# Middle block's sample as half of a sixth pair, path A's low halves split on chip, W_B's sums in pieces, and last gates whose sums are not kept

## The chip, the cores and the metric

The kernel runs on one core of a Trainium2 chip. The metric is the device time of one execution in microseconds (us). Times of the kernel before are from three runs and from one profiled execution.

## What is computed

One layer over 2048 prompt tokens and 64 sample tokens with a state of their own, all in fp32: two paths from one input projection, merged by gates, then an output projection and a gate of 256 extra features.

```python
vA, bA, cA, zA, q, f, iv, zB, gA, gB = split_cols(rms_norm(x, g_pre) @ w_in)
u = cA * vA                                    # path A: a convolution of width 3
yA = (silu(zA) * bA * causal_conv3(u_ext, conv_w)) @ w_a_out
fg = lb + (1.0 - lb) * sigmoid(f)              # path B: 8 heads of 128 x 128
S_new, o = hgrn2_scan(S0, silu(q) * QK_SCALE, 1.0 - fg, iv, log(fg))
yB = (rms(o) * g_onorm * silu(zB)) @ w_b_out
merged = sigmoid(gA) * yA + sigmoid(gB) * yB
x = x + rms_norm(merged @ w_o, g_post)
gate = sigmoid(rms_norm(x, g_ple) @ w_ple_gate)
x = x + (p @ w_ple_proj) * gate
```

The scan goes in chunks of 64 tokens: within a chunk an attention with a causal mask, between chunks a state of 128 x 128 that decays by a factor for each key channel. The outputs are x, the convolution's tails and the states, for prompt and sample apart.

## The kernel before

**Blocks.** The 2112 tokens (prompt 0 to 1407, the 64 sample tokens, then the rest of the prompt) are worked off in three blocks of 768, 704 and 640 tokens. Features stand on the partitions. The middle block holds ten chunks of prompt and, as its eleventh and last, the sample.

**Matrix multiplications.** An fp32 factor is split into a high part (a cast to fp32r) and a low part (the rest), and a product is three multiplications: hi by xhi, hi by xlo, lo by xhi (lines 442, 443, 444 in `sgroup`). `sgroup` makes two columns of weights by two halves of a block with seven products instead of eight. It needs seven weight blocks of 128 x 512: A11, A12 and A22, which are parts of the weights, and four sums S1 to S4. A product is 12 multiplications. Behind each product `hook()` runs one piece of other work, taken from a list of slots.

**Weights.** In the first block `combined` loads the parts, forms the four sums on VectorE (DVE, line 352), makes the casts on ScalarE (ACT) and the low halves on DVE (line 226), and `keep_sum` and `split_w` store the sums (S) and the low halves (low) to HBM. Later blocks read them back: `kept_w` loads a block (raw) and `split_w` makes the cast on ACT and loads the low half, both in the queue of SyncE (SP). `used_later` lists which low halves are stored. `prepare_sums` does the same for weights of later stages, by DMAs of POOL (GpSimd): it loads four blocks, forms S1, S3, S2, S4 and stores each with its low half. For W_B, the weights of path B's output, this runs beside path A of the middle block, one pair of columns in each of the steps j = 3 to 7 (`side`).

**Stages of a block.** Path B (8 heads), then the gates, path A (8 steps j, each with the groups VA/CA and ZA/BA), the two output projections with the merge, W_O and the last gate. The gates' group GB + 6 is the last of the list `fills`; in the middle block it comes first of all, in block 2 behind the preparation of head 5 (`late_gates`).

**A head.** `head_prep` makes two `sgroup`s: forget gate and values (FF, IV), then z and queries (ZB, QQ), with the scan of the logarithms and the keys `ka` and `kb` between. v, the keys `kb` and the output `on` are turned to tokens on partitions: a transposition of 32 x 32 blocks on DVE (line 1054), a write to DRAM by POOL (tv, tk, to; line 1056), a read in another order (line 1061), and for tk a copy on POOL (line 1066). `head_attn` then makes, in slots between the products of the next group: the scores p_a (lines 1111 and 1112), the mask (1120), the update p_u = kt v (1126), the states one after another (1143), the output p_o (1166 and 1168) and its norm. Two chunks of 64 make a pair, and four pairs share a PSUM bank. In the blocks after the first, slots 2 and 3 hold p_a of the two parts, 6 p_u, 8 p_o. The middle block's lone sample chunk goes by itself, in slots 4, 5, 7 and 10, through tiles `lone` and by transpositions on TensorE: of keys and values (1098), and of the output (1193).

**Order.** Instructions of an engine run in the order in which they are recorded; each DMA queue takes its transfers in order as well. The names in the rows below are tiles with a running number: pg is a gemm's PSUM bank, pa one of the attention, r and hf tiles of a whole and a half block, raw, hi, lo and s weight blocks.

Of the kernel before, what the change touches and what calls it, by code (L numbers as in the profile page):

```python
# [18 lines left out]
P = 128  # L19
# [28 lines left out]
def plan():  # L48
# [3 lines left out]
    for size in SIZES:  # L52
# [8 lines left out]
        assert all(g["len"] == 2 * CH for g in groups[:npair])  # L61
        parts = [groups[i : min(i + 4, npair)] for i in range(0, npair, 4)] + [[g] for g in groups[npair:]]
        halves = [dict(t0=t0 + o, off=o, n=size // 2) for o in (0, size // 2)]
        out.append(dict(t0=t0, n=size, runs=runs, npair=npair, parts=parts, groups=groups, segs=halves, last=t0 + size == TOK))
# [29 lines left out]
def hybrid_step(  # L94
# [102 lines left out]
    lone = [const.tile([P, 1, P], F32, tag=f"lone{i}", name=f"lone{i}") for i in range(3)]  # L197

    def constants():
# [9 lines left out]
        for t in atts + lone:  # L209
            V.memset(t, 0.0)  # L210
# [474 lines left out]
    def rstd_of(ms_ap, out_ap, scale, start=0):  # L685
# [3 lines left out]
        powers[:] = [G.tensor_tensor(out_ap, out_ap, mhalf[start : start + shape[0], :].to_broadcast(shape), ALU.pow).ins]  # L689
# [246 lines left out]
    def head_prep(bl, hc, hd, first, hs, before):  # L936
        n, npair = bl["n"], bl["npair"]
        nch, np1 = n // CH, npair * P
        sf, vt = rt(), rt()

        def sink_f(c, h, x, y):
# [9 lines left out]
            into(half(vt, h)[:, n1:], x[:, n1:], None if y is None else y[:, n1:])  # L951
# [5 lines left out]
        lg, b, eq, qx = rt(), rt(), rt(), rt()  # L957
        wrote = [turned("tv", vt, qx, npair)]
# [8 lines left out]
        ka, kb, qe, z = hf(npair * CH), rt(), rt(), rt()  # L967

        def scaled(after):
# [17 lines left out]
            more = npair - 2 * SWAP  # L987
            for lo, hi, to in (
                (0, SWAP, ka3[:, more + 1 :: 2, :]),
                (SWAP, 2 * SWAP, ka3[:, more : npair - 1 : 2, :]),  # L990
                (2 * SWAP, npair, ka3[:, :more, :]),
            ):
                own = slice(2 * lo, 2 * hi, 2)
                V.tensor_tensor(to, chunks(sf)[:, own, :], chunks(lg)[:, own, :], ALU.mult)
                scale = f2[:, lo:hi].unsqueeze(2).to_broadcast([P, hi - lo, CH])
                place = slice(2 * lo + (hi <= SWAP), 2 * hi, 2)
                V.tensor_tensor(chunks(kb)[:, place, :], to, scale, ALU.mult)
# [36 lines left out]
        with behind_all([*wrote, *powers]):  # L1034
            by_token = [in_rows("tv", npair)]
            if before is not None and not first:
                before["ot"] = in_rows("to", npair, before["on"])
            if not first:
                by_token.insert(0, in_rows("tk", npair))
        return dict(  # L1040
            eq=eq, f=f, ka=ka, kb=kb, qe=qe, qx=qx, vt=vt, z=z, by_token=by_token, on=None,
            npair=npair, more=npair - 2 * SWAP, first=first, last=bl["last"], carry=None,
# [26 lines left out]
    def head_attn(ip, gs, d, hd):  # L1069
# [3 lines left out]
        nt, ln = len(gs), gs[0]["len"]  # L1073
        o0, n = gs[0]["off"], nt * ln
        qe, z, att = d["qe"], d["z"], atts[ip]
        single = ln < P
        assert (nt == 2 * SWAP) == (o0 == 0)
        rows = slice(P - ln, P)

        def tile3(i=None):  # L1080
            if single and i is not None:
                return lone[i]
            if nt == 1:
                return small.tile([P, 1, P], F32, tag="one", name=nm("one"), bufs=5)
            return cols3(rt(nt * P), nt)

        def cols(t, g):
            end = g["off"] + ln
# [4 lines left out]
        ready = [] if single else [t[:, o0 // P : o0 // P + nt] for t in d["by_token"]]  # L1093
        for q, src in enumerate((d["kb"], d["vt"])[: 2 - len(ready)]):
            turn_ = ps_attn()
            with placed():
                for i, g in enumerate(gs):
                    T.transpose(turn_[:, i * P : i * P + P], cols(src, g), ident)
            ready.insert(q, tile3(q))
            A.copy(ready[q][rows], cols3(turn_, nt)[rows])  # L1100
        kt, v = ready
        p_a = ps_attn()
        with placed():
            for i, g in enumerate(gs):
                o = g["off"]
                shared = nt == 2 * SWAP
                if not single and (i < SWAP or not shared):
# [4 lines left out]
                T.matmul(p_a[:, i * P + CH : i * P + P], cols(d["kb"], g), qe[:, o + ln - CH : o + ln], start=True, stop=True)  # L1112
        pa3 = cols3(p_a, nt)

        if single:
            V.copy_predicated(att[CH:, :nt, CH:], caus[0][CH:, CH:].unsqueeze(1).to_broadcast([CH, nt, CH]), pa3[CH:, :, CH:])
        else:
            for swapped, lo, hi in ((1, 0, SWAP), (0, SWAP, nt)) if nt == 2 * SWAP else ((0, 0, nt),):
                mask = caus[swapped].unsqueeze(1).to_broadcast([P, hi - lo, P])
                V.copy_predicated(att[:, lo:hi], mask, pa3[:, lo:hi])  # L1120
# [8 lines left out]
        sample = gs[0]["sample"]  # L1129
        if sample:  # L1130
# [657 lines left out]
```

## Time and profile before

| | |
|---|---|
| three runs, median (lowest, highest) | 2547.45 us (2541.86, 2547.89) |
| the profiled execution | 2544.89 us, span 2543.2 us |
| TensorE busy (PE) | 2524.2 us, 99% |
| VectorE (DVE) / ScalarE (ACT) / GpSimd (POOL) busy | 71% / 59% / 18% |
| moved by DMA | 781.01 MB, mean 307 GB/s |

The busy times are those of the span. TensorE's matmuls are pipelined, so the duration of one row (0.32 us) is longer than the distance to the next (0.16 us); what an event costs is read from the next start. In the chain of waits, a DMA is a piece of time in which TensorE's next work waited for a transfer that had been issued at the start shown. In the view of waits, a row gives the total, the number and the longest of one kind.

### The profile page before, as it was taken

The numbers are of one execution on the slowest core, as the hardware profiler recorded it, in microseconds if no ns is written. First come the engines' busy times: TensorE is split into PE (matmuls) and PEld (weight loads), VectorE is DVE, ScalarE is ACT, GpSimd is POOL, SyncE is SP. The second block draws the span as 40 slices with busy tenths as digits, with TensorE's granted clock in tenths as the row PEclk, the third lists the DMA queues.
The fourth block names the chain that finished last, engine by engine and source line by source line (L and its number), as shares of the span: only waits on it lengthen the run. The fifth ranks groups of instructions, "written<-read, shape, count | busy, mean of one in ns | idle before, by whom it ended". The sixth has DMA issues, their size and how long they took to land.

```text
span 2543.2 us, 46984 instructions
## 1 busy us (share of the span) xinstructions
PE 2524.2 (99%) x16022; PEld 2511.2 (99%) x16022; DVE 1796.8 (71%) x3533; ACT 1499.3 (59%) x2940; POOL 462.7 (18%) x809
## 2 busy tenths in 40 slices
PE   9999999999999999999999999999999999999998
PEld 9999999999999999999999999999999999999998
DVE  7889888889868775467774557988347755336967
ACT  6766676554453764466655556567456665446674
POOL 2012121221022022122221221102212221001011
PEclk9999999999999999999999999999999999999999
DMA  8789888999797888988889998989999999999985
GB/s 331 246 291 340 305 297 304 349 354 328 258 345 250 274 288 306 309 286 299 294 298 308 357 380 307 327 289 308 333 306 317 319 337 322 298 299 327 334 270 195
DMA packets 371937, 781.01 MB, mean 307 GB/s; under 512 B 45990, under 2 KB 50912, under 8 KB 371696
## 3 DMA queue, kind: packets, MB, share of 16 engines
q1 hardware_dynamic: 321840, 582.95, 67.0%
q0 software_dynamic: 49856, 195.04, 21.3%
q8 instruction: 126, 2.06, 0.3%
q14 instruction: 115, 0.94, 0.1%
HBM read 562.57 MB, written 215.24 MB: 306 GB/s over the span
## 4 chain that ended last, share of the span: by engine, by line
PE 89%; DMA 4%; issue 3%; DVE 2%; ACT 0%; POOL 0%; SPq 0%; DVEq 0%; POOLq 0%; ACTq 0%
PE pg L442 19%; PE pg L444 19%; PE pg L443 19%; PE pg L593 5%; PE pg L594 5%; PE pg L595 5%; PE pg L632 3%; PE pg L633 3%; PE pg L631 3%; PE pa L1126 1%; PE pa L1166 1%; DMA lo<-low 1%; PE pa L1168 1%; PE pa L1112 1%; DMA s<-low 1%
## 5 line engine op out<-in xcount | busy, mean ns | idle before, releaser
L442 PE MATMUL pg<-r,hi 128*128 128x320 f32 (+2 forms) x3304 | 1078.7, 326 | 0.1
L443 PE MATMUL pg<-r,hi 128*128 128x320 f32 (+2 forms) x3304 | 1067.8, 323 | 0.0
L444 PE MATMUL pg<-r,lo 128*128 128x384 f32 (+2 forms) x2368 | 772.5, 326 | 1.7 <-DMA lo<-low 1.5
L273 ACT CAST hi<-raw 128x512 fp32r<-128x512 f32 x726 | 447.2, 619 | 486.3 <-PE pg L443 188.1
L442 PEld LDWEIGHTS pg<-r,hi 128*128 128x128 f32 x3304 | 621.6, 188 | 0.8 <-ACT hi L226 0.4
L443 PEld LDWEIGHTS pg<-r,hi 128*128 128x128 f32 x3304 | 621.4, 188 | 0.0
L444 PEld LDWEIGHTS pg<-r,lo 128*128 128x128 f32 x2368 | 444.6, 188 | 2.8 <-DMA lo<-low 2.1
L444 PE MATMUL pg<-r,s 128*128 128x320 f32 (+1 forms) x936 | 295.8, 316 | 2.0 <-DMA s<-low 2.0
L594 PE MATMUL pg<-r,hi 128*128 128x320 f32 (+2 forms) x864 | 277.5, 322 | 0.0
L593 PE MATMUL pg<-r,hi 128*128 128x320 f32 (+2 forms) x864 | 274.9, 322 | 0.2 <-ACT r L226 0.2
L226 ACT CAST hi<-raw 128x512 fp32r<-128x512 f32 x252 | 155.4, 621 | 151.5 <-PE pg L443 41.3
L226 DVE TENSOR_TENSOR r<-r,r 128x320 fp32r<-128x320 f32 (+7 forms) x350 | 206.4, 609 | 43.9 <-ACT r L226 42.9
L226 ACT CAST r<-r 128x320 fp32r<-128x320 f32 (+7 forms) x350 | 183.3, 557 | 43.9 <-DVE r L390 9.3
L226 DVE TENSOR_TENSOR lo<-raw,hi 128x512 fp32r<-128x512 f32 x231 | 157.7, 687 | 71.8 <-ACT hi L226 67.8
L595 PE MATMUL pg<-r,lo 128*128 128x352 f32 (+2 forms) x564 | 180.8, 321 | 0.4 <-DMA lo<-low 0.4
L444 PEld LDWEIGHTS pg<-r,s 128*128 128x128 f32 x936 | 176.0, 188 | 2.6 <-DMA s<-low 2.6
L226 ACT CAST hi<-s 128x512 fp32r<-128x512 f32 x160 | 98.9, 620 | 130.1 <-PE pg L443 106.1
L632 PE MATMUL pg<-r,hi 128*128 128x384 f32 (+2 forms) x512 | 167.5, 328 | 0.2 <-DVE r L226 0.2
L631 PE MATMUL pg<-r,hi 128*128 128x384 f32 (+2 forms) x512 | 166.0, 328 | 0.5 <-ACT hi L226 0.3
L594 PEld LDWEIGHTS pg<-r,hi 128*128 128x128 f32 x864 | 162.1, 188 | 1.2 <-DVE r L226 0.8
L593 PEld LDWEIGHTS pg<-r,hi 128*128 128x128 f32 x864 | 161.3, 188 | 1.6 <-ACT r L226 1.2
L456 ACT COPY hf<-pg 128x352 f32<-128x352 f32 (+2 forms) x354 | 157.4, 447 | 1.2 <-PE pg L444 0.8
(393 smaller groups left out, 4134.9 us busy)
## 6 DMA issues: line engine op xcount, KB each, us to landing
raw<-w_blk SPq DMA_DIRECT2D x578, 256.0 KB, 4.5
raw<-S SPq DMA_DIRECT2D x440, 256.0 KB, 4.6
lo<-low SPq DMA_DIRECT2D x421, 256.0 KB, 4.4
s<-low SPq DMA_DIRECT2D x305, 256.0 KB, 4.5
low<-lo SPq DMA_DIRECT2D x275, 256.0 KB, 4.2
S<-s SPq DMA_DIRECT2D x156, 256.0 KB, 4.0
low<-r POOLq DMA_DIRECT2D x50, 256.0 KB, 5.9
r<-w_blk POOLq DMA_DIRECT2D x48, 256.0 KB, 7.3
```

The source lines that it names most:

```text
L226: return A.copy(hi, src).ins, V.tensor_tensor(lo, src, hi.bitcast(F32), ALU.subtract).ins
L273: A.copy(hi, raw)
L442: add(hi[:, k, :], xhi, start=start and k == 0, stop=False)
L443: add(hi[:, k, :], xlo, start=False, stop=False)
L444: last[0] = add(lo[:, k, :], xhi, start=False, stop=k == KH - 1).ins
L456: copied = A.copy(got[n], ps[bank])
L593: add(hi[:, k, :], xhi, start=start and k == 0, stop=False)
L594: add(hi[:, k, :], xlo, start=False, stop=False)
L595: last[0] = add(lo[:, k, :], xhi, start=False, stop=k == KH - 1).ins
L631: T.matmul(ps, hi[:, k % 4, :], xhi[:, c], start=k == ks[0], stop=False)
L632: T.matmul(ps, hi[:, k % 4, :], xlo[:, c], start=False, stop=False)
L633: last[0] = T.matmul(ps, lo[:, k % 4, :], xhi[:, c], start=False, stop=k == ks[-1]).ins
```

## The change

1. The sample chunk becomes the first half of a sixth pair. `plan` makes parts of four and two pairs (the second `mixed`). The tiles that are turned get 768 columns (`turn`); those of the half without tokens are zero (`vt`) or a copy (`kb`). The tiles `lone`, their transpositions and their slots go.
2. In path A, the low halves of A12 and A22 are neither stored nor loaded, but formed on chip in each block.
3. The sums of the gates' group GB + 6 are not stored; the group is formed anew in blocks 1 and 2. `late_gates` goes: in block 2 the group runs behind path B's last preparation.
4. W_B's sums are formed in pieces, one in every fourth slot from slot 24 of the middle block's head 7 on, instead of one pair of columns in a step of `side`.

```diff
-        parts = [groups[i : min(i + 4, npair)] for i in range(0, npair, 4)] + [[g] for g in groups[npair:]]
+        turn = len(groups)
+        parts = [groups[i : i + 4] for i in range(0, turn, 4)]
...
 def used_later(idx, part):
+        if idx < QQ * 8:
+            return part != 1
...
 def keep_sum(name, i1, s):
+        if i1 == GB * 8 + KB - 2:
+            return split_w(s)
...
 def kept_w(i1, i2, name, anew=False, spread=False):
-            return split_w(load_raw(w_blk[keys[name]]), None if anew else keys[name], spread)
+            return split_w(load_raw(w_blk[keys[name]]), None if anew else keys[name], spread or keys[name][0] < QQ * 8 and keys[name][1] == 1)
...
 def head_prep(bl, hc, hd, first, hs, before):
+        odd_end = turn > npair
+        sf, vt = rt(), rt(turn * P)
+        if odd_end:
+            V.memset(vt[:, n - CH : n], 0.0)
...
-        wrote = [turned("tv", vt, qx, npair)]
+        wrote = [turned("tv", vt, staged_v, turn)]
...
+            if odd_end:
+                V.tensor_copy(chunks(kb)[:, nch - 1 : nch + 1, :], ka3[:, more - 1 : more, :].to_broadcast([P, 2, CH]))
...
             if not first:
-                wrote.append(turned("tk", kb, b, npair))
-            if nch % 2:
-                end = slice(nch - 1, nch)
-                V.tensor_tensor(chunks(kb)[:, end, :], chunks(sf)[:, end, :], chunks(lg)[:, end, :], ALU.mult)
+                wrote.append(turned("tk", kb, staged_k, turn))
...
 def head_attn(ip, gs, d, hd):
+                if mixed:
+                    if i == 0:
+                        c = o // CH
+                        to = p_a[:, : 2 * 3 * CH].rearrange("p (g c) -> p g c", c=3 * CH)[:, :, :CH]
+                        T.matmul(to, d["ka"][:, :P], chunks(qe)[:, c : c + 3 : 2, :], start=True, stop=True)
...
+                if g["len"] == P:
+                    T.matmul(p_a[:, i * P + CH : i * P + P], cols(d["kb"], g), qe[:, o + CH : o + P], start=True, stop=True)
...
+        if mixed:
+            V.copy_predicated(att[CH:, nt - 1, CH:], caus[0][CH:, CH:], pa3[CH:, nt - 1, CH:])
...
-        p_t = ps_attn()
-        with placed():
-            for i in range(nt):
-                T.transpose(p_t[:, i * P : i * P + P], on[:, i, :], ident)
-        c = slice(o0, o0 + n)
-        V.tensor_tensor(z[:, c], p_t[:, P - ln : P - ln + n], z[:, c], ALU.mult)
...
 def scale_o(d):
+        if d["turn"] > np_:
+            z = d["z"][:, np_ * P : np_ * P + CH].rearrange("q (i a) -> q i a", a=32)
+            V.tensor_tensor(z, d["ot"][:, np_, 2:], z, ALU.mult)
...
 def path_b(bl, hc, first, kept, fills, hs, lead_sums=None):
-        late_gates = KH + 1 if bl["last"] else None
-            queue, stores[0] = stores[0], SP
             next(fills)
-            stores[0] = queue
-            if hd > 0 if first else hd == late_gates:
+            if first and hd > 0:
                 next(fills, None)
...
-                pairs, one = attn[:2], attn[2:]
-                for slot, steps in enumerate((pairs[:1], pairs[1:], one, one, pairs, one, pairs, (), one)):
+                for slot, steps in enumerate((attn[:1], attn[1:], (), (), attn, (), attn)):
                     at(slot + 2, *steps)
...
+                if hd == NH - 1:
+                    for slot in range(24, 108, 4):
+                        at(slot, piece)
...
-        ahead_of = (*range(W_A, W_A + KH), W_O, W_O + 1) if first else None
+        ahead_of = (*range(W_A, W_A + KH), W_O, W_O + 1) if first else None if bl["last"] else range(W_B, W_B + KH)
...
-        sums_ahead = prepare_sums((W_O + 2, W_O + 3), True) if first else prepare_sums(range(W_B, W_B + KH)) if bi == 1 else iter(())
+        sums_ahead = prepare_sums((W_O + 2, W_O + 3), True) if first else iter(())
```

In a head of the middle block TensorE has the lone chunk's rows between the products of the queries' group, each behind 12 multiplications of a product (left out). Before:

```order
L1098 MATMUL pa_15681<-ident,r_15329 128x128
L1098 MATMUL pa_15684<-ident,r_15122 128x128
L1112 MATMUL pa_15687<-r_15330,r_15329 128x64
L1126 MATMUL pa_15707<-lone_108,lone_107 128x128
L1126 MATMUL pa_15731<-r_15545,r_15550 128x128 x4
L1126 MATMUL pa_15741<-r_15545,r_15550 128x128
L1166 MATMUL pa_15823<-lone_108,att_102 128x128
L1168 MATMUL pa_15823<-s_3753_15710,r_15319 128x128
```

In the change, the same head's p_u and the last rows of its p_o:

```order
L1137 MATMUL pa_15544<-r_15373,r_15378 128x128 x4
L1137 MATMUL pa_15554<-r_15373,r_15378 128x128 x2
L1175 MATMUL pa_15675<-r_15373,att_101 128x128
L1177 MATMUL pa_15675<-s_3674_15561,r_15156 128x128
```

The sample's update is the sixth multiplication behind the pairs' five, and its output the last of the pairs' event.

On DVE, in block 2, these rows stand between the turning of head 7's keys and the queries (L1016) before:

```order
L1054 STREAM_TRANSPOSE r_26297<-r_26309 128x5x4x32
L490 TENSOR_TENSOR r_26310<-hf_26367,hf_26385 128x320
L490 TENSOR_TENSOR r_26310<-hf_26367,pg_26372 128x320
L1028 SCALAR_TENSOR_TENSOR r_26311<-pg_26354,vec,r_26311 128x320
L1015 SCALAR_TENSOR_TENSOR r_26310<-r_26310,r_26506 128x640
L483 TENSOR_TENSOR hf_26502<-hf_26367,pg_26412 128x320
L1016 TENSOR_TENSOR r_26310<-r_26310,r_26298 128x640
```

And in the change, where two more sums of the gates (L355) stand ahead of the first row:

```order
L225 TENSOR_TENSOR lo_26160<-s_26157,hi_26159 128x512
L1064 STREAM_TRANSPOSE r_25922<-r_25934 128x5x4x32
L355 TENSOR_TENSOR s_26169<-s_26163,raw_26145 128x512
L225 TENSOR_TENSOR lo_26166<-s_26163,hi_26165 128x512
L355 TENSOR_TENSOR s_26183<-raw_26151,s_26169 128x512
L225 TENSOR_TENSOR lo_26172<-s_26169,hi_26171 128x512
L1038 SCALAR_TENSOR_TENSOR r_25936<-pg_25979,vec,r_25936 128x320
L493 TENSOR_TENSOR r_25935<-hf_25992,pg_25997 128x320
L493 TENSOR_TENSOR r_25935<-hf_25992,hf_26010 128x320
L486 TENSOR_TENSOR hf_26127<-hf_25992,pg_26037 128x320
L1025 SCALAR_TENSOR_TENSOR r_25935<-r_25935,r_26131 128x640
L1026 TENSOR_TENSOR r_25935<-r_25935,r_25923 128x640
```

Four sums and three low halves of the gates' group have come in among the head's own rows; L1038 and L1026 are what were L1028 and L1016.

In SP's queue, path A of block 2 loads a block and a low half in turns before (A22 is the second w_blk in a row of two, A12 the first):

```order
L236 DMA raw_28105<-S_1952_7800 128x512
L274 DMA lo_28102<-low_7796 128x512
L236 DMA raw_28111<-w_blk 128x512
L274 DMA s_28108<-low_7806 128x512
L236 DMA raw_28117<-w_blk 128x512
L274 DMA lo_28114<-low_7812 128x512
L236 DMA raw_28123<-S_1963_7822 128x512
L274 DMA s_28120<-low_7818 128x512
```

And in the change:

```order
L235 DMA raw_28183<-S_2021_8108 128x512
L275 DMA s_28186<-low_8114 128x512
L235 DMA raw_28189<-w_blk 128x512
L235 DMA raw_28195<-w_blk 128x512
L235 DMA raw_28201<-S_2030_8126 128x512
L235 DMA raw_28315<-w_blk 128x512
L235 DMA raw_28321<-S_2052_8258 128x512
L275 DMA lo_28204<-low_8132 128x512
```

Two low halves of each group have left the queue, 64 loads in blocks 1 and 2; the low halves of the sums and of A11 stay.

More of the change, by code (lines that the diff above doesn't have):

```diff
@@ L60, in plan @@
         npair = sum(g["len"] == 2 * CH for g in groups)
-        assert all(g["len"] == 2 * CH for g in groups[:npair])
-        parts = [groups[i : min(i + 4, npair)] for i in range(0, npair, 4)] + [[g] for g in groups[npair:]]
+        turn = len(groups)
+        assert all(g["len"] == 2 * CH for g in groups[:npair]) and (turn == npair or turn == npair + 1 == 2 * SWAP + 2)
+        parts = [groups[i : i + 4] for i in range(0, turn, 4)]
         halves = [dict(t0=t0 + o, off=o, n=size // 2) for o in (0, size // 2)]
-        out.append(dict(t0=t0, n=size, runs=runs, npair=npair, parts=parts, groups=groups, segs=halves, last=t0 + size == TOK))
+        out.append(dict(t0=t0, n=size, runs=runs, npair=npair, turn=turn, parts=parts, groups=groups, segs=halves, last=t0 + size == TOK))
         t0 += size
@@ L208, in constants @@
         V.memset(keep.rearrange("p (c t) -> p c t", t=CH)[:, :, 0:1], 0.0)
-        for t in atts + lone:
+        for t in atts:
             V.memset(t, 0.0)
@@ L1069, in head_attn, with tile3 @@
     def head_attn(ip, gs, d, hd):
[L1073 to L1076, printed above, removed]
+        nt = len(gs)
+        o0, qe, att = gs[0]["off"], d["qe"], atts[ip]
+        mixed = gs[-1]["len"] < P
         assert (nt == 2 * SWAP) == (o0 == 0)
[L1078 to L1084, printed above, removed]
+        def tile3():
+            if mixed or nt == 1:
+                return small.tile([P, 2, P], F32, tag="one", name=nm("one"), bufs=3)[:, :nt]
             return cols3(rt(nt * P), nt)
         def cols(t, g):
-            end = g["off"] + ln
+            end = g["off"] + g["len"]
             return t[:, end - P : end]
-        ready = [] if single else [t[:, o0 // P : o0 // P + nt] for t in d["by_token"]]
-        for q, src in enumerate((d["kb"], d["vt"])[: 2 - len(ready)]):
+        ready = [t[:, o0 // P : o0 // P + nt] for t in d["by_token"]]
+        if len(ready) == 1:
             turn_ = ps_attn()
@@ L1097, in head_attn @@
                 for i, g in enumerate(gs):
-                    T.transpose(turn_[:, i * P : i * P + P], cols(src, g), ident)
-            ready.insert(q, tile3(q))
-            A.copy(ready[q][rows], cols3(turn_, nt)[rows])
+                    T.transpose(turn_[:, i * P : i * P + P], cols(d["kb"], g), ident)
+            ready.insert(0, tile3())
+            A.copy(ready[0], cols3(turn_, nt))
         kt, v = ready
@@ L1144, in head_attn @@
             cur = ss[:, i, :]
-        if g["end"]:
+            if not g["end"]:
+                continue
             end = small.tile([P, P], F32, tag="state", name=nm("state"), bufs=NH + 1)
@@ L1666, in ready @@
             a_first.extend(narrow(half(t, 0)) for t in a[:KH])
-        path_a(bl, hc, a, first, side(rows, iter(()) if first else sums_ahead), ready)
+        path_a(bl, hc, a, first, side(rows), ready)
         assert not hooks
```

101 lines of the change are left out of this document (46 added, 55 removed).

## The prediction

> **What bounds the kernel now.** First the page's busy times, its clock row and the shares of its chain of waits.
>
> ```profile
> PE 2524.2 (99%) x16022; PEld 2511.2 (99%) x16022; DVE 1796.8 (71%) x3533; ACT 1499.3 (59%) x2940; POOL 462.7 (18%) x809
> PEclk9999999999999999999999999999999999999999
> PE 89%; DMA 4%; issue 3%; DVE 2%; ACT 0%; POOL 0%; SPq 0%; DVEq 0%; POOLq 0%; ACTq 0%
> ```
>
> TensorE is busy for 2524.2 of the 2543.2 us of the span and its clock row is full in every slice. So only two things can move the time: work that TensorE no longer does (or does more of), and its 19 us without work. The other engines count where they make TensorE wait. The view of waits on TensorE says how little of that there is and where this change touches it:
>
> ```profile
> PE pg L444 <- DMA s<-low: 2.0, 2, 1.1
> PE pg L444 <- DMA lo<-low: 1.5, 2, 0.8
> PE pa L1126 <- POOL r L1066: 1.1, 2, 0.8
> ```
>
> All stored low halves together cost 3.5 us; p_u's wait for the turned tk costs 1.1. Removing 111 transfers of 256 KB, as this change does, can therefore bring no more than some 3.5 us, whatever their share of the traffic.
>
> **Part 1, the sample chunk.** The PE timeline of one head of the middle block has all of the chunk's events; gemm rows stand behind each, so that the next start gives an event's length.
>
> ```profile
> 1161.05 0.38 PE L1098 MATMUL pa<-ident,r 128*128 128x128 f32 x2
> 1161.41 0.41 PE L442 MATMUL pg<-r,hi 128*128 128x352 f32 x1
> 1163.44 0.38 PE L1126 MATMUL pa<-lone,lone 128*128 128x128 f32 x2
> 1163.58 0.41 PE L442 MATMUL pg<-r,hi 128*128 128x352 f32 x1
> 1163.82 0.32 PE L443 MATMUL pg<-r,hi 128*128 128x352 f32 x1
> 1163.98 0.32 PE L444 MATMUL pg<-r,lo 128*128 128x352 f32 x1
> 1165.61 1.28 PE L1126 MATMUL pa<-r,r 128*128 128x128 f32 x10
> 1166.64 0.41 PE L442 MATMUL pg<-r,hi 128*128 128x352 f32 x1
> 1168.65 0.38 PE L1166 MATMUL pa<-lone,att 128*128 128x128 f32 x2
> 1169.02 0.41 PE L442 MATMUL pg<-r,hi 128*128 128x352 f32 x1
> 1171.03 0.38 PE L1166 MATMUL pa<-r,att 128*128 128x128 f32 x2
> 1173.17 0.41 PE L442 MATMUL pg<-r,hi 128*128 128x352 f32 x1
> ```
>
> (x2 where the code has one multiplication: these fp32 ones are recorded in two passes.) Gemm rows follow each other at 0.16 us (1163.82 to 1163.98), but the first behind an attention event takes 0.24 (1163.58 to 1163.82), so each event costs 0.08 beside its own length. Removed in a head: the two transpositions with the lone p_a, 1161.05 to 1161.41, 0.36 + 0.08 = 0.44; the lone p_u, 0.14 + 0.08 = 0.22; the lone p_o, 0.37 + 0.08 = 0.45; the single transposition back (L1193), the gap and an estimated 0.02, 0.10. That is 1.21. Added to the pairs' events: a sixth p_u, a fifth of 1165.61 to 1166.64, 0.21; a sixth p_o, a fifth of 1171.03 to 1173.17, 0.43; 64 columns more in the second p_a, some 0.05. That is 0.69. Net 0.52 us in a head, times 8: **-4.2**. TensorE's work, not a wait, so nothing can hide this gain; bounds -3.4 and -4.8 (0.1 us in a head, what a gap and a pitch are read to).
>
> What it costs: tv, tk and `to` are turned through DRAM with six pairs, 384 KB instead of 320, and p_u needs all of tk where it did not need the sample's part. The page's DMA issues have the same kind of transfer in both sizes:
>
> ```profile
> tv<-r POOLq DMA_DIRECT2D x16, 320.0 KB, 4.1
> tk<-r POOLq DMA_DIRECT2D x16, 320.0 KB, 5.2
> r<-tv POOLq DMA_DIRECT2D x16, 320.0 KB, 7.0
> r<-tk POOLq DMA_DIRECT2D x16, 320.0 KB, 6.9
> tv<-r POOLq DMA_DIRECT2D x8, 384.0 KB, 3.9
> r<-tv POOLq DMA_DIRECT2D x8, 384.0 KB, 5.2
> ```
>
> From one end, the larger one is not longer at all (3.9 against 4.1): growth 0. From the other, in proportion to bytes, (5.2 + 6.9) x 0.2 = 2.4. I take 0.45, near the end that the rows of the same transfer show, because those of 384 KB ran in another block. The Trainium skill's page "DMA: Bandwidth & Descriptors", section "Anatomy of one DMA — SWDGE (gpsimd) path", fits one such transfer by about 2.0 us and a microsecond for each 436 KB: 0.15 us more for 64 KB, so 0.3 for the way out and back, and the stall below would be 0.65 instead of 0.8. Its 2.8 us for 320 KB is far below the 6.9 measured here between other transfers, so the row is used.
>
> The slack of that way is read from the end of POOL's copy to the next p_u, here in the sixth and the eighth head:
>
> ```profile
> 1264.75 0.72 POOL L1066 COPY r<-r 128x640 f32<-128x640 f32 x1 [7.26 <-DMA r<-tk]
> 1265.79 0.38 PE L1126 MATMUL pa<-r,r 128*128 128x128 f32 x2
> 1330.07 0.71 POOL L1066 COPY r<-r 128x640 f32<-128x640 f32 x1 [6.25 <-DMA r<-tk]
> 1332.62 0.27 PE L1126 MATMUL pa<-r,r 128*128 128x128 f32 x1
> ```
>
> 0.32 us in the sixth, 1.84 in the eighth (1332.62 less 1330.78), and by the same reading 1.9 to 4.0 in the others. p_u now comes 0.6 us earlier, since 0.44 + 0.22 ahead of it are gone and 0.05 is new; the copy of 768 columns takes a fifth of 0.71 more, say 0.1. With 0.45 of growth the slack shrinks by 1.15: only the sixth head stalls, **+0.8**. Bounds: 0.4 at no growth (shrunk by 0.7); at 2.4 the loss is 3.1, which is 2.8 in the sixth and 1.3 or less in each of the others, together some 7.9. The sample's last multiplication of z is new and waits for `to` on DVE; DVE, busy for 71% of the span, has the time, and I take it at nothing (bound: its wait added to the same slack, which B below holds).
>
> **Part 2, path A's low halves and W_B's sums in pieces.** TensorE's two late loads in the middle block's path A stand in the chain of waits (first fence, start and length); the table by stretches shows the load on the DMA engines there (second fence; columns: length, busy PE, PEld, DVE, ACT, POOL, clock, DMA share, GB/s).
>
> ```profile
> 1437.24 12.66 DMA lo<-low
> 1472.53 11.69 DMA s<-low
> ```
>
> ```profile
> 470.00:570.00 100.00, 99.76 (x572) 99.09 (x571) 85.04 (x147) 55.83 (x124) 30.16 (x50) 1.00 0.97 347
> 1440.00:1480.00 40.00, 39.21 (x244) 38.81 (x243) 23.22 (x43) 19.06 (x37) 12.89 (x29) 1.00 1.03 390
> 2150.00:2350.00 200.00, 200.00 (x1363) 200.00 (x1362) 94.02 (x180) 106.42 (x211) 11.31 (x29) 1.00 0.92 308
> ```
>
> Loads of this kind took 12.66 and 11.69 where POOL's bursts for W_B's sums filled the DMA engines (share 1.03). Of the 14 loads that a pair of weight columns needs in path A (seven blocks, their words and low halves), two go. The pieces start at j = 1 instead of 3, so the same bursts stand about twice as far apart. TensorE idles 40 - 39.21 = 0.79 us in the stretch with the first of them, and the second reaches into the next. I take both stalls, of the four in the waits on low halves, as gone, 0.9 for lo and 1.3 for s (somewhat over the longest single waits, 0.8 and 1.1, which leave out the slower start behind): **-2.2**. Bounds 0 (the bursts still collide) and -3.5 (all waits for low halves go). The added 64 subtractions on DVE, 0.69 us each, are 44 us; they are taken at nothing, since DVE is busy for 23 of 40 and 94 of 200 us in such stretches. Without that cover each late one costs up to 0.69, but block 0 does the same splits at 85% DVE (first row) and TensorE is at 99.8% there. The 4 + 32 low stores fewer in block 0: nothing, as they only fill a queue behind which no wait of note stands.
>
> **Part 3, the last gates.** In block 2 their four sums are formed on DVE, with four low halves, and the group no longer stands at head 5 but behind head 7's preparation; the order has four sums and three lows ahead of the three instructions that release TensorE there. Prices and positions:
>
> ```profile
> 1048.57 0.69 DVE L352 TENSOR_TENSOR s<-s,raw 128x512 f32<-128x512 f32 x1
> 1049.18 0.52 DVE L462 TENSOR_TENSOR hf<-hf,pg 128x352 f32<-128x352 f32 x1
> L226 DVE TENSOR_TENSOR lo<-raw,hi 128x512 fp32r<-128x512 f32 x231 | 157.7, 687 | 71.8 <-ACT hi L226 67.8
> 2100.67 0.89 DVE L1188 TENSOR_TENSOR r<-pa,ms 128x512 f32<-128x512 f32 x2 [1.04 <-POOL ms L689]
> 2109.49 0.82 DVE L1016 TENSOR_TENSOR r<-r,r 128x640 f32<-128x640 f32 x1
> 2111.97 0.27 PE L1111 MATMUL pa<-r,hf 128*128 128x128 f32 x1
> ```
>
> Seven such instructions at the pitch of 0.61 (1048.57 to 1049.18) are 4.3 us; the three lows wait for ACT's cast, 71.8 / 231 = 0.31 each, 0.9 together: DVE comes 5.2 us later to L1016, which p_a needs. In before it ends at 2110.31 and p_a starts at 2111.97, a slack of 1.66, and DVE's idle time ahead of it, 1.04 us for POOL's result at L1188, has no added instruction in it. **+3.5**, in part already at the group's third product, which waits for a PSUM bank that L1028 frees. Queued behind the late instructions are the masks and the state updates of head 7, which come as late as their TensorE events, so they add nothing. Bounds: 0, if the sums fit into DVE's idle time (block 1 forms these same four sums at its start without a wait on DVE), and 5.9, if all eight stand ahead (8 x 0.61 + 4 x 0.31 - 1.66 = 4.4) and the first sum waits an estimated 1.5 for its weights, a third of a load of 4.4 us. Heads 5 and 6 of block 2 lose the group of gates whose time TensorE spent while their tk was on its way; heads without it stalled 0.8 and 0.3 (the 1.1 in the waits): **+0.4**, bounds 0 and 1.
>
> **Sum.** -4.2 + 0.8 - 2.2 + 3.5 + 0.4 = **-1.7 us** against the profiled execution's 2544.9 us (span 2543.2 and 1.7 around it): 2543.2. The median of the three runs shown is 2547.45, 2.6 above that execution, and they spread from 2541.86 to 2547.89. I forecast 2544.
>
> **Rivals.**
> A, the last gates are hidden: DVE's order lets the sums slip ahead, and every wait for a low half goes. Speaks for it: block 1's gates. Against: the order has the sums inside head 7's chain. -4.2 - 3.5 + 0.4 (no growth) + 0 = -7.3: 2537.6.
> B, slower: tk's way through DRAM becomes what the middle block's heads wait for. Place: p_u of heads 0 to 7; price: growth by bytes, 7.9 in place of 0.8; it decides from a loss of slack of 2.1 us on, where the stalls reach 2.5 and the sum turns positive. For it: the slack of 0.32. Against: the rows of 384 KB. -1.7 + 7.1 = +5.4: 2550.3.
> C, the pieces don't thin out the bursts: the order still has the four sums of a pair of columns within some seven rows of DVE. The 2.2 stay: 2545.4.
> D, POOL's copy of tk is held up by DVE, which now has 60 more instructions:
>
> ```profile
> L1066 POOL COPY r<-r x16: 713/715/1103, 1094.0 to 2119.7; 128x640 f32<-128x640 f32 x16
> ```
>
> One of 16 took 0.39 longer than the median; if all did, 16 x 0.39 = 6.2 at most: 2549.4. The Trainium skill's page "SBUF — State Buffer", section "Who interferes with whom", has DVE with two SBUF inputs and a reading GpSimd instruction lock each other out for whole instructions, which would be this mechanism; that 15 of 16 copies show nothing of it speaks against more than a rare case.
>
> **How the numbers follow.** My forecast gets 0.53, A 0.20, B 0.13, C 0.10, D 0.04. About 0.3%, 7.6 us, is what a measurement of this kernel tells from no change. A ends just inside of it and half of its spread lies beyond (0.10), and a tenth of the rest with gains I don't see: faster 0.20. B and D need another late term, the upper bound of the gates (+2.4), to pass 7.6, to which I add unseen stalls behind DVE: slower 0.13. Same 0.67. The range takes in A and B with the runs' spread: 2536 to 2552; the forecast's own is 2540 to 2548.
>
> **What would show it.** Right: TensorE's busy time in a middle head of some 32.9 us instead of 33.4; no L444 wait for lows between 1430 and 1490; in block 2 a gap of 3 to 4 us on TensorE around head 7's p_a, released by DVE; DVE's busy time up by some 40 us. Wrong: p_u in the middle block waiting on POOL in more than two heads (B), no gap at head 7 (A), or low loads of path A's sums still landing 10 us after issue (C).

## The result, and the profile after

The changed kernel takes 2537.35 us in the median of 8 runs (2535.46 to 2538.84), the kernel before 2543.64 us in the median of 8 (2541.50 to 2547.89). The ratio is 0.9971 with a 95% interval of 0.9961 to 0.9981: 0.29% less. That is a gain clear of the interval, but inside the 0.3% that the prediction counts as no change. (The 2547.45 given ahead of the prediction is the median of three of the runs before.) The profiled execution has a span of 2536.1 us, against 2543.2.

First the page's busy times of the changed kernel, and those of its waits on TensorE that the change touches (total, times, longest):

```profile
PE 2518.9 (99%) x15982; PEld 2506.1 (99%) x15982; DVE 1841.7 (73%) x3593; ACT 1495.8 (59%) x2916; POOL 455.1 (18%) x801
```

```profile
PE pg L447 <- DMA s<-low: 1.6, 1, 1.6
PE pg L445 <- DVE r L1038: 1.6, 1, 1.6
PE pa L1122 <- DVE r L1026: 1.1, 1, 1.1
PE pa L1137 <- POOL r L1076: 0.8, 1, 0.8
PE pg L598 <- DMA lo<-low: 0.4, 1, 0.4
```

TensorE has 5.3 us less work and 17.2 us without any, 1.8 less than before. DVE has 45 us more. Waits for low halves fell from 3.9 us to 2.0, and two waits for DVE are new, at the lines that the prediction named.

Where the 7.1 us of the two profiled executions lie is read by laying the same product of both PE timelines side by side:

| up to | change against before, us | in this stretch |
|---|---|---|
| end of block 0's products (about 890) | -0.8 | -0.8 |
| first head of the middle block (about 1083) | -1.8 | -1.1 |
| end of its heads (about 1377) | -6.3 | -4.4 |
| end of its path A (about 1500) | -8.3 | -2.0 |
| block 2's first head (about 1884) | -7.9 | +0.4 |
| end of block 2's heads (about 2149) | -5.5 | +2.4 |
| end of its path A (about 2309) | -6.2 | -0.7 |
| last instruction | -7.1 | -0.8 |

**The sample's pair.** The starts of two following p_a's in the middle block, before (L1111) and after (L1122):

```profile
1121.98 0.38 PE L1111 MATMUL pa<-r,hf 128*128 128x128 f32 x2
1155.41 0.27 PE L1111 MATMUL pa<-r,hf 128*128 128x128 f32 x1
```

```profile
1119.55 0.38 PE L1122 MATMUL pa<-r,hf 128*128 128x128 f32 x2
1152.41 0.38 PE L1122 MATMUL pa<-r,hf 128*128 128x128 f32 x2
```

A head takes 32.86 us instead of 33.43. The sixth pair's price is in the two events that grew, p_u and p_o (the next gemm's start ends each):

```profile
1161.93 1.50 PE L1137 MATMUL pa<-r,r 128*128 128x128 f32 x12
1163.18 0.41 PE L445 MATMUL pg<-r,hi 128*128 128x352 f32 x1
1167.13 0.38 PE L1175 MATMUL pa<-r,att 128*128 128x128 f32 x2
1169.72 0.41 PE L445 MATMUL pg<-r,hi 128*128 128x352 f32 x1
```

p_u takes 1.25 us (1.03 before), p_o 2.59 (2.14).

**tk's way.** The DMA issues of the middle block's heads (1080 to 1380 us), before with 320 KB and in the change with 384:

```profile
tk<-r POOLq DMA_DIRECT2D x8, 320.0 KB, 4.6
r<-tk POOLq DMA_DIRECT2D x8, 320.0 KB, 6.9
```

```profile
tk<-r POOLq DMA_DIRECT2D x8, 384.0 KB, 4.3
r<-tk POOLq DMA_DIRECT2D x8, 384.0 KB, 7.4
```

The way out did not grow, the way back grew by 0.5 us. The other profiles agree: there the way back takes 6.8 to 6.9 us with 320 KB (part 1 undone, parts 2 and 4 alone) and 7.3 to 7.6 with 384. The sixth head's slack, from POOL's copy to p_u:

```profile
1259.23 0.82 POOL L1076 COPY r<-r 128x768 f32<-128x768 f32 x1 [6.50 <-DMA r<-tk]
1260.51 0.28 PE L1137 MATMUL pa<-r,r 128*128 128x128 f32 x1
```

It is 0.46 us, more than the 0.32 before; no head of the middle block waited. In the three other profiles with 320 KB the sixth head's slack is 1.4 to 1.5, so the 0.32 was one execution's.

**The last gates.** The DVE timeline of block 2's last head:

```profile
2086.08 0.68 DVE L225 TENSOR_TENSOR lo<-s,hi 128x512 fp32r<-128x512 f32 x1
2086.68 1.32 DVE L1064 STREAM_TRANSPOSE r<-r 128x640 f32<-128x640 f32 x1
2087.92 0.65 DVE L355 TENSOR_TENSOR s<-s,raw 128x512 f32<-128x512 f32 x1
2088.49 0.68 DVE L225 TENSOR_TENSOR lo<-s,hi 128x512 fp32r<-128x512 f32 x1
2089.09 0.68 DVE L355 TENSOR_TENSOR s<-raw,s 128x512 f32<-128x512 f32 x1
2089.69 0.68 DVE L225 TENSOR_TENSOR lo<-s,hi 128x512 fp32r<-128x512 f32 x1
2090.30 0.54 DVE L1038 SCALAR_TENSOR_TENSOR r<-pg,vec,r 128x320 f32<-128x320 f32 x1
```

They run back to back at the pitch of 0.60, without a wait for ACT, and TensorE's two waits (1.6 on L1038, 1.1 on L1026) follow.

### The profile page after: what moved, and what is told of

It is laid out like the page before. It is cut to its first block, busy times and chain, and to the rows that moved or that the text cites. A ratio compares the mean times of both kernels' runs of the same rounds, so it can differ in the third digit from the quotient of the medians.

```text
span 2536.1 us, 46699 instructions
## 1 busy us (share of the span) xinstructions
PE 2518.9 (99%) x15982; PEld 2506.1 (99%) x15982; DVE 1841.7 (73%) x3593; ACT 1495.8 (59%) x2916; POOL 455.1 (18%) x801
## 5 line engine op out<-in xcount | busy, mean ns | idle before, releaser
L447 PE MATMUL pg<-r,s 128*128 128x352 f32 (+1 forms) x924 | 292.3, 316 | 1.6 <-DMA s<-low 1.6
L225 DVE TENSOR_TENSOR lo<-raw,hi 128x512 fp32r<-128x512 f32 x263 | 179.8, 687 | 76.7 <-ACT hi L225 73.7
```

The costliest lines, as they stand in the source:

```text
L225: return A.copy(hi, src).ins, V.tensor_tensor(lo, src, hi.bitcast(F32), ALU.subtract).ins
L447: last[0] = add(lo[:, k, :], xhi, start=False, stop=k == KH - 1).ins
```

## The experiments

Ratios are against the kernel before on the same chip; the change itself has 0.9971 (0.9961 to 0.9981).

### The parts undone, one by one

Part 1 undone. The edit puts the lone chunk's lines back (as in the diff above, with signs turned):

```diff
...
-                for slot, steps in enumerate((attn[:1], attn[1:], (), (), attn, (), attn)):
+                for slot, steps in enumerate((pairs[:1], pairs[1:], one, one, pairs, one, pairs, (), one)):
...
```

> The changed kernel with part 1 undone: the middle block's sample goes by itself again (lone tiles, 320 KB turned); parts 2 to 4 stay. Theory (part 1 takes work off TensorE and its longer way through DRAM costs no wait): a head of the middle block is 33.4 us again instead of 32.84, 4.4 us over eight heads, so about 2541.7 us against the change's 2537.35. Rival (the gain came from the lighter DMA traffic, and part 1 gives back at other waits what it saves): within 1 us of 2537.35.

2542.57 us, ratio 0.9997 (0.9988 to 1.0006). Its p_a's on the PE timeline:

```profile
1121.15 0.38 PE L1115 MATMUL pa<-r,hf 128*128 128x128 f32 x2
1154.58 0.38 PE L1115 MATMUL pa<-r,hf 128*128 128x128 f32 x2
```

33.43 us again, so the theory holds. The profile's other differences from the change's, none over 1.2 us, cancel but for 0.3.

Part 2 undone:

```diff
-        if idx < QQ * 8:
-            return part != 1
...
-            return split_w(..., spread or keys[name][0] < QQ * 8 and keys[name][1] == 1)
+            return split_w(..., spread)
```

> The changed kernel with part 2 undone: path A's low halves of A12 and A22 are stored and loaded again. Theory (they, not the pieces, made the two loads of the middle block's path A late): TensorE waits again for a low half in that path A, 2.1 us, and block 2's path A takes back the 0.7 us it lost without a stall; 2540 to 2540.5. Rival (the pieces alone removed those waits): no wait for a low half in that path A, at most 0.7 + 0.7 us more, 2538 to 2539.

2542.21 us, ratio 0.9994 (0.9985 to 1.0003). That is 4.9 us above the change, with intervals that don't overlap, so part 2 is worth something; but neither the theory's size (2.7 to 3.2) nor its place holds. TensorE works for 189.80 of 190 us in that path A, and no low half is late. In the profiled execution the time lies in block 0 (1.8 us, below) and at the last gates (4.3 us, with half the clock there, further below); other stretches give 2 us back.

Part 3 undone (sums stored and read, group at head 5):

```diff
-        if i1 == GB * 8 + KB - 2:
-            return split_w(s)
...
+        late_gates = KH + 1 if bl["last"] else None
...
+            queue, stores[0] = stores[0], SP
             next(fills)
+            stores[0] = queue
...
-            if first and hd > 0:
+            if hd > 0 if first else hd == late_gates:
...
```

> The changed kernel with part 3 undone: the last gates' sums are stored in the middle block by SP's queue and read in block 2 at head 5. Theory (the sums in DVE's order cost TensorE 2.85 us at head 7, while the stores in SP's queue cost 1.1 at the start of the middle block): the gap at head 7 goes, the wait of about 1 us near 1050 comes back: 1.7 us less, about 2535.6. Rival (the gap at head 7 is there for another reason, or moves): 2537 to 2538.5.

2535.68 us, ratio 0.9967 (0.9955 to 0.9980). The stretch of the last head by the table of windows (length, PE, PEld, DVE, ...), with part 3 undone and in the change:

```profile
2080.00:2100.00 20.00, 20.00 (x146) 20.00 (x145) 16.27 (x40) 14.75 (x24) 5.13 (x8) 1.00 0.88 291
```

```profile
2080.00:2100.00 20.00, 17.34 (x121) 16.84 (x120) 16.86 (x38) 11.10 (x20) 5.37 (x8) 1.00 0.67 222
```

The gap is gone, and a wait of 0.9 us for a low half near 1051 is there, as the theory said. The intervals of the two kernels overlap; the gap is shown by the traces, the 1.7 us of the medians are not.

Part 4 undone (sums a pair of columns at a time, `side` as before):

```diff
-            ... else None if bl["last"] else range(W_B, W_B + KH)
+            ... else None
...
-        def side(rows):
+        def side(rows, sums_):
...
+                if j >= 3:
+                    next(sums_, None)
```

> The changed kernel with part 4 undone: W_B's sums are formed a pair of columns at a time at j = 3 to 7 of the middle block's path A. Theory (with two low loads of a group gone the queue has room for the bursts): no wait of TensorE for a load there, within 0.7 us of 2537.35. Rival (the pieces removed the waits): waits of about 2 us near 1440 to 1480, 2539 to 2539.6.

2539.77 us, ratio 0.9987 (0.9978 to 0.9996), a median 2.4 us above the change's, with overlapping intervals. The median lies just above the rival's 2539 to 2539.6. But the profiled execution, the shortest of its runs (2537.03), has no wait in that path A, as the theory said; what the longer ones waited for it can't show. What part 4 is worth beside part 2 stays open.

### The parts alone

Part 1 alone, its lines of the diff above put into the kernel before:

```diff
+        parts = [groups[i : i + 4] for i in range(0, turn, 4)]
...
+                for slot, steps in enumerate((attn[:1], attn[1:], (), (), attn, (), attn)):
```

> The kernel before with part 1 alone (the sample as half of a sixth pair). Theory (TensorE's work in the middle block's heads, nothing given back): heads of 32.8 instead of 33.4 us, 4.4 us less than before, ratio 0.9983. Rival (the longer way through DRAM takes it back at p_u): heads of 33.2 us or more, ratio above 0.9992.

2540.49 us, ratio 0.9986 (0.9978 to 0.9995): 3.6 us less. Its p_a's:

```profile
1124.80 0.38 PE L1118 MATMUL pa<-r,hf 128*128 128x128 f32 x2
1157.65 0.38 PE L1118 MATMUL pa<-r,hf 128*128 128x128 f32 x2
```

32.85 us. The theory holds from both sides.

Part 2 alone:

```diff
+        if idx < QQ * 8:
+            return part != 1
...
+            return split_w(..., spread or keys[name][0] < QQ * 8 and keys[name][1] == 1)
```

> The kernel before with part 2 alone (path A's low halves of A12 and A22 on chip). Theory (either part 2 or part 4 is enough to remove the late loads of the middle block's path A): no wait for a low half between 1320 and 1540, 2.1 us less, and 0.8 less in block 0, whose stores of low halves go: ratio 0.9988. Rival (the late loads go only with both parts): a wait of 0.9 us or more there, ratio 0.9995 or above.

2540.51 us, ratio 0.9988 (0.9980 to 0.9997): 3.1 us less (3.6 by the medians). The ratio is the theory's, and no wait for a low half stands between 1320 and 1540. But the profiled execution (2542.01) has one of 2.0 us in block 0, near 748, with the granted clock at 0.50 for 3.4 us behind it.

Part 4 alone:

```diff
+                if hd == NH - 1:
+                    for slot in range(24, 108, 4):
+                        at(slot, piece)
```

> The kernel before with part 4 alone (W_B's sums in pieces from head 7 on). Theory (either part is enough): no wait for a low half in the middle block's path A, 2.1 us less, ratio 0.9992. Rival (both are needed): a wait of 0.9 us or more there, ratio 0.9997 or above.

2543.54 us, ratio 1.0000 (0.9991 to 1.0009): no gain that could be measured. The middle block's path A in the kernel before, then with part 1 alone and with part 4 alone:

```profile
1346.00:1536.00 190.00, 188.08 (x1167) 187.39 (x1166) 95.31 (x183) 103.96 (x209) 44.54 (x99) 1.00 0.99 354
```

```profile
1346.00:1536.00 190.00, 189.38 (x1175) 188.73 (x1174) 96.77 (x187) 103.43 (x210) 44.71 (x99) 1.00 1.00 358
```

```profile
1346.00:1536.00 190.00, 190.00 (x1181) 189.93 (x1181) 97.15 (x188) 104.74 (x211) 46.12 (x99) 1.00 1.00 359
```

With part 1 alone, low halves and bursts are those of the kernel before, the DMA share is 1.00, and still the two late loads are not there (its 0.6 us stand at the window's start, a wait for ACT near 1358). So the code alone does not make TensorE wait there, and a second profile of the kernel before, which could say how often it does, is not on record.

What the code does change is how late the loads land. Of the low halves that SP loaded in this window, counted in the traces, 7 of 95 took over 10 us from issue to landing before (the longest 12.7) and 5 of 95 with part 1 alone (11.9). With part 4 alone it is 2 of 96 (10.3), with part 2 alone 3 of 69 (10.9), in the change 2 of 67 (10.8). So either part seems enough to make late landings rarer, each by one profile; whether one of them becomes a wait of TensorE differs from profile to profile.

What part 2 does bring shows in block 0. The stretch around 560 us, before and in the change:

```profile
550.00:575.00 25.00, 24.76 (x140) 24.09 (x140) 18.65 (x35) 13.93 (x30) 2.83 (x5) 1.00 0.91 320
```

```profile
550.00:575.00 25.00, 25.00 (x144) 25.00 (x143) 23.28 (x44) 14.77 (x32) 3.53 (x6) 1.00 0.87 313
```

With part 4 alone TensorE has 24.17 us there, with part 1 alone 24.50, with part 2 undone 24.00; with part 2 alone 25.00. What DVE waits for, with part 4 alone (one instruction, and the group over block 0's path A) and with part 2 alone:

```profile
558.05 0.69 DVE L226 TENSOR_TENSOR lo<-s,hi 128x512 fp32r<-128x512 f32 x1 [4.59 <-DMA low<-lo]
...
L226 DVE TENSOR_TENSOR lo<-s,hi 128x512 fp32r<-128x512 f32 x54 | 37.2, 689 | 18.8 <-DMA low<-lo 9.9 <-ACT hi L226 8.7
```

```profile
L226 DVE TENSOR_TENSOR lo<-s,hi 128x512 fp32r<-128x512 f32 x54 | 37.2, 690 | 15.6 <-ACT hi L226 15.4
```

A tile of a low half is free only when its store has read it. With part 2 two of seven aren't stored, and DVE's 9.9 us of waiting for stores (9.0 in the kernel before) go. DVE's idle time before these instructions falls by 3.2 us only (18.8 to 15.6), since it then waits longer for ACT's casts. On TensorE it is 0.2 to 1.0 us in this stretch, in all four profiles with the stores and in none of the ten without.

### The last gates' place and sums

Sums stored and read, the place as in the change:

```diff
-        if i1 == GB * 8 + KB - 2:
-            return split_w(s)
```

> The changed kernel with the last gates' sums and their low halves stored in the middle block by POOL's queue and read in block 2; the group stays behind head 7's preparation. Theory (the four sums and three lows in DVE's order make the gap at head 7; the place does not; and SP's stores made the wait at the middle block's start): no gap at head 7 of block 2 and no wait near 1050, so 2.85 us less than the change, about 2534.5 us. Rival (the place behind head 7 makes the gap by itself): a gap of 2 us or more stays, about 2537.

2536.10 us, ratio 0.9966 (0.9953 to 0.9979). TensorE is busy for all 20 us from 2080 to 2100: the sums make the gap, not the place. The wait near 1050 stayed (1.0 us) with POOL's stores. Profiles without any store of these sums have it as well (part 1 undone, 0.8), others not (the change): the store queue is not its cause.

Sums formed anew as in the change, at the place of the kernel before:

```diff
+        late_gates = KH + 1 if bl["last"] else None
...
-            if first and hd > 0:
+            if hd > 0 if first else hd == late_gates:
...
```

> The changed kernel with the last gates' sums formed anew as in the change, but at head 5 of block 2, where the kernel before had the group. Theory (DVE has the sums inside a head's chain in either place): a gap of 1.5 to 3 us at head 5, about the change's 2537. Rival (the place decides): no gap, about 2534.5.

2539.36 us, ratio 0.9981 (0.9972 to 0.9991). TensorE's stretch at head 5:

```profile
2020.00:2040.00 20.00, 16.11 (x106) 15.35 (x105) 15.59 (x34) 10.62 (x20) 4.13 (x6) 1.00 0.72 252
```

3.9 us, more than the 2.7 at head 7: the theory's gap (2.3), and late low halves behind it (1.6). The median is 2.4 us above the forecast.

Both edits together, so that only the stores' queue differs from the kernel with part 3 undone:

> The changed kernel with the last gates' sums stored by POOL's queue in the middle block and read in block 2 at head 5: no sums inside a head's chain, and the group's 13.5 us back between tk and its use in head 5. Theory (the sums on DVE are the only cost of part 3): no gap, the time of the two kernels with kept sums, 2535.5 to 2536.5, at best 0.5 less for the tk of heads 5 and 6. Rival (SP's stores in the kernel with part 3 undone cost 1 us at the middle block's start): a further 1 us less, 2534.5.

2538.75 us, ratio 0.9980 (0.9971 to 0.9989). There is no gap at the gates, but three waits for low halves elsewhere (1052, 1064, 1703), 3.0 us together, though the profiled execution is the shortest of its runs (2536.61). Theory and rival both forecast less time. It isn't better than the other two with kept sums (0.9967 and 0.9966), and no version here is shown to beat the change.

### What a longer gap costs

```diff
-                V.tensor_tensor(s, x, y, op)
+                for _ in range(1 + (1 if name == "S2" and i1 == GB * 8 + KB - 2 and len(formed) == 1 else 0)):
+                    V.tensor_tensor(s, x, y, op)
...
```

`formed` counts how often the group's sums were formed, so that the extra instruction comes in block 2 alone.

> The changed kernel with S2 of the last gates formed twice in block 2, one instruction of DVE more (0.61 us) inside head 7's chain. Theory 1 (a gap costs its length): TensorE's gap there grows by 0.6, and the time by 0.6 us. Theory 2 (a gap a little longer than the change's 1.6 us drops the granted clock to 0.5 for some us, as the profiles of the undone parts show): a stretch at 0.5 behind the gap, and 2 to 4 us more in all, 2539.5 to 2541.

2541.86 us, ratio 0.9989 (0.9980 to 0.9999): 4.5 us above the change by the medians, more than either theory said. In the profiled execution the wait on L1038 (L1041 in this kernel) is 1.1 us, the clock stays at 1.00, and two low halves of the same group come late (the longer one by 1.6 us):

```profile
PE pg L450 <- DMA lo<-low: 3.1, 4, 1.6
PE pg L448 <- DVE r L1041: 1.1, 1, 1.1
```

That wait is shorter than the change's 1.6 because the edit also moved other instructions in DVE's order:

```profile
2090.39 0.65 DVE L356 TENSOR_TENSOR s<-s,raw 128x512 f32<-128x512 f32 x1
2090.95 0.69 DVE L225 TENSOR_TENSOR lo<-s,hi 128x512 fp32r<-128x512 f32 x1
2091.55 0.69 DVE L356 TENSOR_TENSOR s<-s,raw 128x512 f32<-128x512 f32 x1
2092.16 0.55 DVE L1041 SCALAR_TENSOR_TENSOR r<-pg,vec,r 128x320 f32<-128x320 f32 x1
2092.62 0.68 DVE L356 TENSOR_TENSOR s<-raw,s 128x512 f32<-128x512 f32 x1
2093.22 0.69 DVE L225 TENSOR_TENSOR lo<-s,hi 128x512 fp32r<-128x512 f32 x1
```

S2 stands twice ahead of L1041, but S4 (`raw,s`) and the low half behind it, which the change has ahead of that instruction, now follow it. So this run did not lengthen the gap, and theory 1 was not tested by it.

> The changed kernel with S2 of the last gates formed four times in block 2, three instructions of DVE more (1.83 us) inside head 7's chain. Theory 1 (a gap costs its length): 1.8 us more. Theory 2 (long gaps drop the clock): 1.8 us and 2 to 4 us more for the stretch at 0.5, 2541 to 2543; the stretch not much longer than with one more, if its length is fixed.

The same edit, with three instructions more in place of one. 2542.06 us, ratio 0.9990 (0.9981 to 1.0000); no more than with one. The median lies in theory 2's range, but here too two of the three added instructions stand behind L1041. In the profiled execution (2545.86, the longest of its runs) the waits of this group are 5.4 us together, and the granted clock falls to 0.50 twice; whether it does in the shorter runs isn't shown. The expectation rested on what the profiles of the undone parts 1, 2 and 4 show; here part 2 undone (the clock is the third number from the end):

```profile
2092.00:2094.00 2.00, 0.38 (x3) 0.41 (x4) 2.00 (x5) 0.76 (x2) 0.92 (x2) 1.00 1.00 299
2094.00:2096.00 2.00, 2.00 (x13) 1.84 (x11) 1.51 (x4) 1.65 (x4) 0.83 (x2) 0.76 1.00 318
2096.00:2098.00 2.00, 1.38 (x6) 1.13 (x6) 2.00 (x4) 1.12 (x3) 0.00 (x0) 0.50 1.06 398
2098.00:2100.00 2.00, 2.00 (x10) 2.00 (x11) 0.88 (x3) 0.00 (x0) 0.00 (x0) 0.50 1.02 361
2100.00:2102.00 2.00, 2.00 (x10) 2.00 (x9) 0.88 (x3) 0.00 (x0) 0.00 (x0) 0.53 0.87 317
```

Behind a wait of 2.4 us TensorE runs at half clock for some 6.8 us, by estimate 3 us on top of the gap itself.

## Why the prediction held, and where its terms were off

The sign of the sum was right, and the time, 2537.35, lies in the range of 2536 to 2552, near its lower end. The forecast of 2544 was 6.7 us too high, and the forecast's own 2540 to 2548 did not hold the time; it was the room left for rival A that did. On the profiled executions the forecast was -1.7 and the change -7.1. That A's 2537.6 comes nearest is chance: A has no gap at head 7 and no wait for a low half, and neither came true.

- **Part 1, -4.2.** Right: -4.4 in the traces of the heads, with 0.22 and 0.45 for the grown p_u and p_o (forecast 0.21 and 0.43). Alone it gives 0.9986, undone the gain is gone.
- **tk's way, +0.8.** Too high: nothing in the change, 0.3 us or less in the other profiles with part 1. The growth of 0.45 was about right (0.5 on the way back, none on the way out), and so was the loss of slack: over the eight heads it fell by 1.05 us in the mean, against the 1.15 expected. Wrong was to take the sixth head's slack of 0.32, read from one execution, as the kernel's. B is out: tk's way grew by 0.5 us, not by the 2.4 that its price rests on.
- **Part 2 and 4, -2.2.** The number appears in the table (-2.0), but that is in part luck. The step "I take both stalls ... as gone" read two waits of one execution as the kernel's: with part 1 alone they are absent too. The mechanism, late landings made rarer, is seen in the loads, yet part 4 alone brings nothing measurable. C's own sign, low loads that land over 10 us after issue, is nearly gone (2 of 67, against 7 of 95). (The prediction's 3.5 us for all low halves leaves out 0.4 on L595, and its bound counted no wait behind the stores.)
- **"The 4 + 32 low stores fewer in block 0: nothing, as they only fill a queue behind which no wait of note stands."** Wrong. The stores hold the tiles of the low halves; DVE waits for them and TensorE behind DVE, 0.2 to 1.0 us. The waits on TensorE name DVE there, not the store; the store is found one step further back, in the row of L226. Part 2 alone is worth 0.9988, 3.1 us; of this the stores explain up to 1, and where the rest lies no trace settled. Loads that come late less often would fit, and so does the spread of 11 runs each (8.8 us with part 1 alone, 8.3 with part 4 alone, 5.5 with part 2 alone, 3.2 with parts 2 to 4), but this doesn't show it: a profile shows one execution.
- **Part 3, +3.5.** Right in mechanism, place and releasers; 2.7 in the waits (2.9 with the slower starts behind). The 0.9 us for ACT's casts was the part that was not there. A is out: the gap is in every profile with the sums on DVE, and in none without.
- **Heads 5 and 6, +0.4.** Not seen: the waits of p_u are 0.8 in all, 1.1 before.
- **D** is out: the eight copies of 768 columns take about 0.82 us, 0.11 over the 0.71 before and as the prediction had it, and nothing waits for them.
- The remaining stretches, -1.1 at the start of the middle block, +0.4, -0.7 and -0.8, were in no term. The first two are landings of low halves that come and go among kernels with the same code there: the wait of 0.7 near 1052 is absent in the change, and the one near 1701 is 1.6 instead of 0.9 us. The last is a wait of 1.3 us for DVE (L733) near 2498 in the profile before, which is 0.2 to 0.6 in all thirteen others. The -0.7 in block 2's path A comes back (0.5 to 0.7) in every profile with parts 1 and 2 and is nothing with part 1 or part 4 alone; its cause is open.

## What to carry to other kernels

Where one engine is busy 99% of the time, its own instructions removed are the term to trust: they came out to 0.2 us of 4.4, while waits for DMAs, of 0 to 3 us, came and went between profiles of kernels with the same code at that place. A wait, or a slack, belongs in a sum only if a second profile, or a second kernel with the same code at that place, has it too. Compare a transfer's sizes within the same block of the work, and look at the order that an edit leaves on the engine before reading its time. And a store is not free because nobody reads it: ask who waits for the tile that it holds.

## What the runs showed of the hardware

A gap on TensorE can cost more than its length: behind waits of 1.8 (part 4 undone), 2.0 (part 2 alone) and 2.4 us (parts 1 and 2 undone) the granted clock was 0.50 for 3.4 to 6.8 us, while it stayed at 1.00 behind 1.6 us in the change, behind 2.0 near 1703 with one sum more, and behind 2.3 with the sums at head 5. So length alone doesn't decide.

The traces' clock records show more. Within a run every change of the clock lies a whole multiple of 3.41 us after the first (part 4 undone: 5.2, 2090.8, 2094.2 us). Cut the span on that grid: ahead of five of the six drops inside the kernels, one stretch of 3.41 us held 1.8 to 2.4 us without a matmul. Stretches at the full clock with 1.6 us or less were followed by the full clock, but for one (1.4 us, with three sums more). The half clock lasted one or two such stretches. The 2.3 us at head 5 are cut by the grid into 1.2 and 1.1, the 2.0 near 1703 into 0.8 and 1.3. So what counts seems to be how much of one stretch is idle; no run varies that by itself.

The Trainium skill's page "TensorE: Matmul & The Clock Gate", section "What's actually happening", has the clock halve after an idle window of about 3.4 us whose phase runs freely. The grid agrees with such a window; that little more than half of one was enough doesn't, and there the measurement decides.
